# A Hymba layer on one core: halved RMS statistics, ScalarE sums for the first norm, respaced sums of the down weights and a hand-set GpSimd order

## The chip, the cores and the metric

The kernel is one launch on one core of a Trainium2 chip. The time is device microseconds from the start to the end of an execution, and lower is better. Engines are named as the profile names them: PE is TensorE (matmuls), DVE is VectorE, ACT is ScalarE, POOL is GpSimd, and SP issues the DMAs, one after the other in the order of its queue.

## What is computed

One layer on 1024 tokens of width 1024, in float32. Four steps follow one another: embedding norm and mixing (stick-breaking attention of 8 heads beside causal pooling of 4 windows), the first layer norm, a squared-ReLU feed-forward of width 4096 with the second norm, and a gated embedding with the third.

```python
x = layer_norm(x, emb_ln_g, emb_ln_b)
proj = x @ w_in; q, k, v, u = split(proj, [512, 1024, 1536])
o = stick_breaking_attention(q, k, v)              # 8 heads of 64
o = o * rsqrt(mean(o * o, per head) + 1e-6) * attn_out_g
pooled = multiscale_pool(u, w_pool, pool_scale)    # windows 2, 4, 8, 16
x = layer_norm(2**0.25 * x + concat(o, pooled) @ w_out, ln1_g, ln1_b)
h = square(relu(x @ w_up)) @ w_down
x = layer_norm(2**0.25 * x + h, ln2_g, ln2_b)
x = layer_norm(2**0.25 * x + sigmoid(x @ w_gate) * (p @ w_ple), ln3_g, ln3_b)
```

## The kernel before

A value enters a matmul as a high and a low part (`split`: ACT casts the high part at L65, DVE or POOL subtracts it at L66), and a product is three matmuls (`mm3`, L69 to L71). The stages follow one another in time.

**Attention, 110 to 384 us.** There are 64 tiles: 4 pairs of heads `pr`, 2 heads `j`, 8 blocks `t` of 128 queries. The loop over n has an order of PE that is written by hand. `weigh` (two z matmuls, two sigmoids on ACT at L398 and L399, a scan on DVE at L400, a multiply and a memset on POOL at L403 and L404) runs three tiles ahead of `turn` (transposes of the weights `aa`, L126, split into `ath` and `atl`) and, on every second tile, `gather` (matmuls `o`, L429). Between them stands the fill: projections `pq` in steps of three matmuls, and the pooling groups, which `pool_group` computes: matmuls `pp`, a scaled copy `y` on ACT (L494), 1 to 4 shifted adds `s` on POOL (L499), and the result `pooled` on DVE (L503 to L507). RATES says how much fill goes beside a tile: 0.37 for the first 48, 0.6 for the others. When a pair is complete its output gets its RMS norm: `rms_square` (one ACT square of 1024 columns, L441), `rms_stats` (matmuls `pm` L447, ACT L450, POOL power L451, POOL copy into `ms` L453) and `rms_apply` (transposes `pb` L460, DVE multiply L462). The fourth pair's stand after the loop, with the last fill around them. Pooled groups and pairs go to DRAM (`mspill`) and come back as `mraw`.

**Output weights, 384 to 484 us.** Three rounds take 3, 3 and 2 blocks of 128 tokens. Each round loads 8 row blocks of `w_out` through two slots: DMA into `wraw`, cast `wh` on ACT, remainder `wl` on DVE or POOL by `takes`, then matmuls `acc`. Round 0 also splits the mixed values (`mix`). After a round, each row block gets its first norm: `xr` from `acc` on DVE (L820), `bn_stats` and its aggregate on DVE (L97, L99, L101), a power on POOL (L103), two passes on DVE (L110, L113), transposes, a copy `xval` and splits (`normed`), and a store `rspill`.

**Start of the up phase, 484 to 530 us.** From here on the order of all engines is written by hand. Rows 6 and 7 get their norm (`finish_rows`, `norm_apply`) between the first products.

**Up phase, 530 to 810 us.** Sixteen groups `g` of seven products (`up`, 12 matmuls each; Strassen's way of seven). Beside each group, sums of the second weights are made for the phase behind: `down_fetch(m)` loads two tiles `draw`, `down_sums(m)` makes four sums on POOL (L574), `down_out(m)` stores them as `tspill`. All three are for group m = g, but group 3 does two, so that m runs one ahead from there. The two `draw` slots are shared, so the fetch of m+1 waits until the stores of m have landed. SP also stores the results `hid` (`hspill`) and loads the up weights `uraw`.

**Down phase, 810 to 1130 us, and the gate, to the end.** The gate phase has norms whose statistics are made on ACT (L1186 to L1189).

Of the kernel before, what the change touches and what calls it, by code (L numbers as in the profile page):

```python
# [8 lines left out]
F32 = mybir.dt.float32  # L9
# [25 lines left out]
def hymba_layer(ctx: ExitStack, tc: tile.TileContext, x, p, emb_g, emb_b, w_in, attn_g, w_pool,  # L35
# [70 lines left out]
    def norm_apply(src, dst, g, b, stats, done=None):  # L106
# [5 lines left out]
        for cs in parts:  # L112
            V.scalar_tensor_tensor(out=dst[:, cs], in0=dst[:, cs], scalar=rs, in1=b[:, cs],  # L113
                                   op0=ALU.mult, op1=ALU.add)
            if done:
                done(cs)

# [248 lines left out]
    RATES = (0.37, 0.6)  # L366
# [72 lines left out]
    def rms_square(pr):  # L439
        sq[pr] = slot("ra", "sq")  # L440
        A.activation(out=sq[pr], in_=oraw[pr], func=AF.Square)  # L441

    def rms_stats(pr):

        pm = bank("b6", "pm")[:, 0:2 * NT]
        for i in range(NT):
            T.matmul(pm[:, 2 * i:2 * i + 2], lhsT=sq[pr][:, i * P:(i + 1) * P], rhs=hm,  # L447
                     start=True, stop=True)
        rs = small.tile([P, 2 * NT], F32, name="rms", bufs=2)
        A.activation(out=rs, in_=pm, func=AF.Identity, bias=eps)  # L450
        G.tensor_tensor(out=rs, in0=rs, in1=mhalf, op=ALU.pow)  # L451
        ms[pr] = slot("K", "ms")
        G.tensor_copy(out=ms[pr].rearrange("p (n d) -> p n d", d=HD),  # L453
                      in_=rs.unsqueeze(2).broadcast_to([P, 2 * NT, HD]))

    def rms_apply(pr, c):
        cs = slice(c * CH, (c + 1) * CH)
# [4 lines left out]
        V.scalar_tensor_tensor(out=oraw[pr][:, cs], in0=oraw[pr][:, cs],  # L462
# [59 lines left out]
    with tc.manual_schedule(engines={mybir.EngineType.PE}):  # L522
        for n in range(-AHEAD, len(tiles)):
# [11 lines left out]
            else:  # L535
# [21 lines left out]
    def mix(k):  # L557
        both = big("mix")
        mixh[k], mixl[k] = both[:, 0:S], both[:, S:2 * S]
        raw = pooled[0] if k == 4 else oraw[3] if k == 3 else None  # L560
# [37 lines left out]
    def normed(i, tps):  # L598
# [4 lines left out]
        xval[i] = slot("ra" if i < 6 else "K", "xval")  # L603
# [177 lines left out]
    for r0 in range(0, NT, 3):  # L781
# [35 lines left out]
        for i in tiles:  # L817
# [4 lines left out]
            layer_norm(xr[i], xr[i], g1, b1)  # L822
# [122 lines left out]

    with tc.manual_schedule(engines=ALL):
# [3 lines left out]
        def finish_rows(i):  # L950
# [4 lines left out]
            stats[i] = norm_stats(xr[i])  # L955
# [32 lines left out]
        norm_apply(xr[6], xr[6], g1, b1, stats[6])  # L988
# [343 lines left out]
```

## Time and profile before

| | |
|---|---|
| Median of 3 runs | 1240.09 us (1237.65 to 1240.2) |
| Profiled execution | 1238.67 us, of which its span 1236.7 us |
| PE busy | 1163.7 us, 94% |
| DVE busy | 903.1 us, 73% |
| ACT busy | 599.2 us, 48% |
| POOL busy | 520.3 us, 42% |
| PE's granted clock, mean | 0.976 of 2.4 GHz |

The page gives busy time over the whole span, and it is a mean over stages with different limits. PE is near full in most of the 40 slices of the page, and shows lower digits and a lower clock in few. A busy PE at half clock (1.2 GHz) counts as busy, so idle time and clock have to be read together, stretch by stretch.

### The profile page before, as it was taken

What the parts mean: (1) busy time and instruction counts of PE and PEld (TensorE: products, weight loads), DVE (VectorE), ACT (ScalarE), POOL (GpSimd) and SP (SyncE); (2) the same over time, 40 slices, a digit from 0 to 9 for tenths busy, and PEclk for the clock granted to TensorE, in tenths of its full rate; (3) what the DMA queues carried; (4) which work ended last, traced back from release to release, by engine and by line L of the source; (5) the groups of instructions that cost most, each with busy time, mean ns of one, the idle gap of its engine ahead of it and who ended that gap; (6) DMA issues with size and microseconds to landing.
All of it is one profiled execution on the core that took longest, in us unless ns stands there. A gap on an engine that the chain in (4) does not pass through costs nothing.

```text
span 1236.7 us, 15529 instructions
## 1 busy us (share of the span) xinstructions
PE 1163.7 (94%) x5520; PEld 964.1 (78%) x5520; DVE 903.1 (73%) x1114; ACT 599.2 (48%) x1038; POOL 520.3 (42%) x368
## 2 busy tenths in 40 slices
PE   7999988899997998699899999999999999998997
PEld 5877877787876876588688888878888888887886
DVE  7735878796865678868576776768888887788565
ACT  5425756675644244454446455466333343335653
POOL 3211443354752236633342332336645564465332
PEclk9999999999997999799899999999999999999999
DMA  9824121121226363378778877799666655643122
GB/s 347 291 115 136 27 61 60 43 60 43 71 83 242 120 243 132 102 253 263 238 256 278 269 252 261 253 378 394 231 220 196 214 175 169 208 138 118 68 78 76
DMA packets 123580, 221.48 MB, mean 179 GB/s; under 512 B 9456, under 2 KB 64240, under 8 KB 123504
## 3 DMA queue, kind: packets, MB, share of 16 engines
q1 hardware_dynamic: 123504, 220.50, 52.4%
q8 instruction: 43, 0.70, 0.2%
q14 instruction: 33, 0.27, 0.1%
HBM read 148.12 MB, written 70.25 MB: 177 GB/s over the span
## 4 chain that ended last, share of the span: by engine, by line
PE 71%; DVE 10%; ACT 6%; DMA 5%; issue 5%; POOL 2%; SPq 1%; DVEq 0%; ACTq 0%; POOLq 0%
PE pd L69 8%; PE pd L71 7%; PE pd L70 7%; PE pu L70 6%; PE pu L71 6%; PE pu L69 6%; PE tp L126 3%; PE pq L69 3%; PE pq L70 3%; PE pq L71 2%; PE acc L70 2%; PE o L429 2%; DVE rr L400 2%; PE acc L71 2%; PE acc L69 2%
## 5 line engine op out<-in xcount | busy, mean ns | idle before, releaser
L574 POOL TENSOR_TENSOR draw<-draw 128x512 f32<-128x512 f32 x64 | 97.1, 1517 | 180.1 <-DMA draw<-in_w_down_dram 177.5
L890 DVE TENSOR_TENSOR xres<-xres,pd 128x512 f32<-128x512 f32 x208 | 137.4, 680 | 45.4 <-PE pd L71 44.5
L574 POOL TENSOR_TENSOR dop<-draw,dop 128x1024 fp32r<-128x1024 f32 (+1 forms) x48 | 112.1, 2355 | 125.2 <-ACT dop L866 107.1
L866 ACT CAST dop<-draw 128x1024 fp32r<-128x1024 f32 (+1 forms) x96 | 81.3, 905 | 134.8 <-DVE xres L890 51.4
L69 PE MATMUL pd<-dop 128*128 128x512 f32 x320 | 125.1, 391 | 2.0 <-DVE xres L890 1.9
L70 PE MATMUL pd<-dop 128*128 128x512 f32 x320 | 124.8, 390 | 0.1
L71 PE MATMUL pd<-dop 128*128 128x512 f32 x320 | 124.6, 389 | 0.0
L574 DVE TENSOR_TENSOR dop<-draw,dop 128x1024 fp32r<-128x1024 f32 (+1 forms) x48 | 85.6, 1784 | 3.6 <-ACT dop L866 3.6
L751 ACT COPY hid<-pu 128x512 f32<-128x512 f32 x48 | 28.2, 588 | 120.8 <-PE pu L71 69.0
L69 PE MATMUL pq<-xh,wh 128*128 128x512 f32 x192 | 77.9, 406 | 0.8 <-DVE ul L66 0.8
L400 DVE TENSOR_TENSOR_SCAN rr<-rr,diag 128x640 f32<-128x640 f32 (+3 forms) x32 | 71.3, 2228 | 9.5 <-ACT rr L398 8.6
L403 POOL TENSOR_TENSOR aa<-aa,rr 128x639 f32<-128x639 f32 (+3 forms) x32 | 56.9, 1779 | 48.4 <-DVE rr L400 48.4
L70 PE MATMUL pq<-xl,wh 128*128 128x512 f32 x192 | 76.7, 399 | 0.0
L71 PE MATMUL pq<-xh,wl 128*128 128x512 f32 x192 | 76.5, 398 | 0.0
L69 PEld LDWEIGHTS pd<-dop 128*128 128x128 f32 x320 | 60.0, 188 | 16.6 <-DVE xres L890 3.2
L574 DVE TENSOR_TENSOR hid<-pu,hid 128x512 f32<-128x512 f32 x48 | 33.0, 688 | 52.7 <-PE pu L71 37.8
L70 PEld LDWEIGHTS pd<-dop 128*128 128x128 f32 x320 | 60.1, 188 | 13.0 <-POOL dop L574 0.8
L71 PEld LDWEIGHTS pd<-dop 128*128 128x128 f32 x320 | 60.1, 188 | 12.5
L65 ACT CAST wh<-wraw 128x1024 fp32r<-128x1024 f32 x36 | 38.0, 1056 | 53.9 <-PE acc L70 26.2
L66 DVE TENSOR_TENSOR atl<-tp,ath 128x512 fp32r<-128x512 f32 (+2 forms) x96 | 50.7, 546 | 15.4 <-ACT ath L65 14.6
L70 PE MATMUL acc<-wl,mix 128*128 128x512 f32 x128 | 51.7, 404 | 4.2 <-POOL wl L66 4.2
L574 DVE TENSOR_TENSOR hid<-hid,hid 128x512 f32<-128x512 f32 x48 | 53.8, 1145 | 0.6
(253 smaller groups left out, 3359.3 us busy)
## 6 DMA issues: line engine op xcount, KB each, us to landing
hspill<-hid SPq DMA_DIRECT2D x48, 512.0 KB, 4.9
draw<-hspill SPq DMA_DIRECT2D x48, 512.0 KB, 6.0
uraw<-in_w_up_dram SPq DMA_DIRECT2D x32, 512.0 KB, 5.8
draw<-in_w_down_dram SPq DMA_DIRECT2D x32, 512.0 KB, 4.7
tspill<-draw SPq DMA_DIRECT2D x64, 256.0 KB, 4.2
wraw<-in_w_out_dram SPq DMA_DIRECT2D x24, 512.0 KB, 3.6
draw<-in_w_down_dram SPq DMA_DIRECT2D x48, 256.0 KB, 5.1
wraw<-in_w_in_dram SPq DMA_DIRECT2D x16, 512.0 KB, 4.9
```

The costliest lines, as they stand in the source:

```text
L65: A.copy(out=h, in_=src)
L66: (eng or V).tensor_tensor(out=l, in0=src, in1=h.bitcast(F32), op=ALU.subtract)
L69: T.matmul(ps, lhsT=lh, rhs=rh, start=start, stop=False, **kw)
L70: T.matmul(ps, lhsT=lh, rhs=rl, start=False, stop=False, **kw)
L71: T.matmul(ps, lhsT=ll, rhs=rh, start=False, stop=stop, **kw)
L126: T.transpose(tp[:, j * P:(j + 1) * P], src[:, (k0 + j) * P:(k0 + j + 1) * P], ident)
L400: V.tensor_tensor_scan(out=rr[:, 0:n][:, ::-1], data0=rr[:, 0:n][:, ::-1], data1=diag[:, S - n:S][:, ::-1], initial=0.0, op0=ALU.mult, op1 ...
L403: G.tensor_tensor(out=aa[:, 0:n - 1], in0=aa[:, 0:n - 1], in1=rr[:, 1:n], op=ALU.mult)
L574: eng.tensor_tensor(out=o, in0=i0, in1=i1, op=op)
L751: A.copy(out=quarter(g, name), in_=ups[g, "A"])
L866: A.copy(out=h, in_=raw)
L890: V.tensor_tensor(out=xres[i][:, cs], in0=xres[i][:, cs], in1=src, op=ALU.add)
```

## The change

In the attention, the RMS norm of each pair is done in two halves of 512 columns, the first after block 3 and the second after block 7 of the second head. The square comes one tile later, the statistics two, the multiply four. Of the fourth pair, the second half's `pm` and `pb` fall behind the first `acc` matmuls, and `mix(3)` is split by halves. RATES[1] goes from 0.6 to 0.8. POOL's order in the attention is written by hand. The first norm's statistics are made on ACT by `row_stats` (a sum by Identity, a mean, a sum by Square, a variance; POOL's power), with `xval` as scratch, and `bn_stats` go. In the up phase the sums of group m start every sixth product up to m = 7 and every seventh from there, and stores and the next fetch follow three products later. `act_stats` and `act_apply` of the gate phase call the new helpers.

```diff
+    def row_stats(src, unused, tag):
+        s1, nm, s2, var, rs = [small.tile([P, 1], F32, name=nme, tag=nme + tag)
+                               for nme in ("s1", "nm", "s2", "va", "ra")]
+        A.activation(out=unused, in_=src, func=AF.Identity, accum_out=s1)
+        A.activation(out=nm, in_=s1, func=AF.Identity, scale=-1.0 / D)
+        A.activation(out=unused, in_=src, func=AF.Square, bias=nm, accum_out=s2)
+        A.activation(out=var, in_=s2, func=AF.Identity, scale=1.0 / D, bias=lneps)
+        G.tensor_tensor(out=rs, in0=var, in1=mhalf[:, 0:1], op=ALU.pow)
+        return nm, rs
+    def row_apply(src, stats, g, b, step, cs=slice(0, D)):
...
-    RATES = (0.37, 0.6)
+    RATES = (0.37, 0.8)
...
+    def rms_square(pr, c):
+        if pr not in sq:
+            sq[pr], ms[pr] = slot("ra", "sq"), slot("K", "ms")
+        A.activation(out=sq[pr][:, half(c)], in_=oraw[pr][:, half(c)], func=AF.Square)
...
-    with tc.manual_schedule(engines={mybir.EngineType.PE}):
+    with tc.manual_schedule(engines={mybir.EngineType.PE, mybir.EngineType.Pool}):
...
-                if k.j == 1 and k.t == NT - 1:
-                    rms_square(k.pr)
-                    later.setdefault(n + 2, []).append((rms_stats, k.pr))
-                    later.setdefault(n + 8, []).append((rms_apply, k.pr, 0))
-                    later.setdefault(n + 10, []).append((rms_apply, k.pr, 1))
-        fill.run(4)
-        rms_stats(3)
+                if k.j == 1 and k.t in (3, 7):
+                    c = k.t // 4
+                    for m, f in ((1, rms_square), (2, rms_stats), (4, rms_apply)):
+                        later.setdefault(n + m, []).append((f, k.pr, c))
         fill.finish()
-        rms_apply(3, 0)
-        rms_apply(3, 1)
+        for n in sorted(later):
+            for f, *args in later[n]:
+                if f is not rms_apply:
+                    f(*args)
...
+        if k == 3:
+            for c in range(2):
+                if c:
+                    rms_apply(3, 1)
+                split(oraw[3][:, half(c)], mixh[k][:, half(c)], mixl[k][:, half(c)])
+            return
...
-            layer_norm(xr[i], xr[i], g1, b1)
+            xval[i] = slot("ra", "xval")
+            stats1 = row_stats(xr[i], xval[i], "1")
+            for step in range(2):
+                row_apply(xr[i], stats1, g1, b1, step)
...
+    sums_at = {6 * m if m < 8 else 7 * (m - 1): m for m in range(NG)}
+
+    def weight_sums(g, n):
+        n += 7 * g
+        if n in sums_at:
+            down_sums(sums_at[n])
+        if n - 3 in sums_at:
+            m = sums_at[n - 3]
+            down_out(m)
+            if m + 1 < NG:
+                down_fetch(m + 1)
...
-            stats[i] = norm_stats(xr[i])
+            xval[i] = slot("K", "xval")
+            stats[i] = row_stats(xr[i], xval[i], "1")
...
-                down_sums(m)
+                weight_sums(g, 0)
...
-            if m < NG:
-                down_out(m)
-            if m + 1 < NG:
-                down_fetch(m + 1)
+            weight_sums(g, 2)
...
-            if g == 3:
-                down_sums(4)
+            weight_sums(g, 5)
```

PE at the end of the attention, before: the low-part matmuls of the last gather, a fill step, the last pooling group, then both RMS steps of the fourth pair.

```order
L429 MATMUL o<-atl,vs 128x256 x7
L69 MATMUL pq<-xh,wh 128x512
L70 MATMUL pq<-xl,wh 128x512
L71 MATMUL pq<-xh,wl 128x512
L69 MATMUL pp<-uh,wph 128x512
L70 MATMUL pp<-ul,wph 128x512
L71 MATMUL pp<-uh,wpl 128x512
L69 MATMUL pp<-uh,wph 128x512
L70 MATMUL pp<-ul,wph 128x512
L71 MATMUL pp<-uh,wpl 128x512
L447 MATMUL pm<-hm,sq 128x2 x8
L460 MATMUL pb<-ident,ms 128x128 x8
```

After, from the statistics of the fourth pair's first half to the first `acc`: tiles 62 and 63 are transposed in one run.

```order
L474 MATMUL pm<-hm,sq 128x2 x4
L149 MATMUL tp<-ident,aa 128x128 x15
L452 MATMUL o<-ath,vs 128x256 x7
L452 MATMUL o<-ath,vs 128x128
L452 MATMUL o<-atl,vs 128x128
L452 MATMUL o<-atl,vs 128x256 x7
L485 MATMUL pb<-ident,ms 128x128 x4
L69 MATMUL acc<-wh,mix 128x512
```

What moved: 14 fill steps and the last two pooling groups went ahead of tile 61's transposes, and half of `pm` and `pb` went behind, so that no fill stands from there to the first `acc`.

POOL at the same place, before: tile 63's multiply (1023 columns) with the adds of the last two pooling groups, then the power and the copy.

```order
L403 TENSOR_TENSOR aa<-aa,rr 128x1023
L499 TENSOR_TENSOR s_3453<-s_3450 128x1020
L499 TENSOR_TENSOR s_3644<-y 128x1023
L499 TENSOR_TENSOR s_3647<-s_3644 128x1022
L499 TENSOR_TENSOR s_3736<-y 128x1023
L451 TENSOR_TENSOR rms<-rms,mhalf 128x16
L453 COPY ms<-rms 128x1024
```

After:

```order
L426 TENSOR_TENSOR aa<-aa,rr 128x1023
L427 MEMSET aa 128x1
L524 TENSOR_TENSOR s_3619<-y 128x1023
L524 TENSOR_TENSOR s_3622<-s_3619 128x1022
L524 TENSOR_TENSOR s_3690<-y 128x1023
L478 TENSOR_TENSOR rms<-rms,mhalf 128x8
L479 COPY ms<-rms 128x512
L478 TENSOR_TENSOR rms<-rms,mhalf 128x8
L479 COPY ms<-rms 128x512
L66 TENSOR_TENSOR wl<-wraw,wh 128x1024
```

What moved: the third add of the 8-window group is done earlier, three adds in a row stand between tile 63's multiply and the first power, and power and copy come in two halves.

ACT in the second round of the output weights, before: casts of the weights, then the copies and splits of row 0.

```order
L65 CAST wh<-wraw 128x1024 x11
L606 COPY xval<-tp 128x512
L65 CAST b11h<-tp 128x2x128
L606 COPY xval<-tp 128x512
L65 CAST b11h<-tp 128x2x128
```

After, with the statistics of rows 0 to 2 between the casts:

```order
L65 CAST wh<-wraw 128x1024 x3
L125 ACTIVATE xval,s_4057<-xr 128x1024
L65 CAST wh<-wraw 128x1024
L126 ACTIVATE nm<-s_4057 128x1
L125 ACTIVATE xval,s_4095<-xr 128x1024
L127 ACTIVATE xval,s_4059<-xr,nm 128x1024
L125 ACTIVATE xval,s_4133<-xr 128x1024
L126 ACTIVATE nm<-s_4095 128x1
L128 ACTIVATE va<-s_4059,lneps 128x1
L126 ACTIVATE nm<-s_4133 128x1
L65 CAST wh<-wraw 128x1024
```

What moved: six passes of 1024 columns, and their small ones, now stand on ACT around casts on which the round's matmuls wait.

SP in groups 2 to 4 of the up phase, before, from the store of group 2's second pair of results (`hid_5261`; `hid_5281` is its third, `hid_5157` and `hid_5233` are group 3's first and fourth):

```order
L74 DMA hspill<-hid_5261 128x1024
L74 DMA uraw<-in_w_up_dram 128x8x128
L74 DMA hspill<-hid_5281 128x1024
L74 DMA tspill<-draw 128x512 x4
L74 DMA draw<-in_w_down_dram 128x1024 x2
L74 DMA hspill<-hid_5157 128x1024
L74 DMA hspill<-hid_5233 128x512
L74 DMA tspill<-draw 128x512 x4
L74 DMA draw<-in_w_down_dram 128x1024 x2
L74 DMA uraw<-in_w_up_dram 128x8x128
```

After (`hid_5305` and `hid_5325` are group 2's second and third, `hid_5193` and `hid_5273` group 3's first and fourth):

```order
L74 DMA uraw<-in_w_up_dram 128x8x128
L74 DMA tspill<-draw 128x512 x4
L74 DMA draw<-in_w_down_dram 128x1024 x2
L74 DMA hspill<-hid_5305 128x1024
L74 DMA uraw<-in_w_up_dram 128x8x128
L74 DMA hspill<-hid_5325 128x1024
L74 DMA hspill<-hid_5193 128x1024
L74 DMA hspill<-hid_5273 128x512
L74 DMA tspill<-draw 128x512 x4
L74 DMA draw<-in_w_down_dram 128x1024 x2
L74 DMA uraw<-in_w_up_dram 128x8x128
```

What moved: the stores of m = 3 and the fetch of m = 4 stand ahead of group 2's second and third stores, and between the stores of m = 3 and of m = 4 there are now four stores and a load of up weights, where there were two stores.

## Rows read from the trace of the kernel before

**Rows 1.** Stretches: us, busy of PE, PEld, DVE, ACT, POOL (x instructions), PE's clock, DMA share.

```profile
349.99:384.65 34.66, 24.91 (x132) 20.68 (x130) 16.45 (x26) 14.05 (x28) 16.60 (x9) 0.86 0.56 192
418.00:484.00 66.00, 61.17 (x285) 49.08 (x285) 53.35 (x75) 27.08 (x43) 33.79 (x17) 1.00 0.57 199
506.00:530.00 24.00, 17.11 (x60) 13.44 (x59) 19.24 (x25) 14.44 (x26) 15.20 (x10) 0.64 0.47 156
610.00:622.00 12.00, 7.71 (x20) 5.69 (x21) 8.27 (x9) 7.00 (x11) 2.82 (x3) 0.57 0.80 281
622.00:810.00 188.00, 188.00 (x831) 155.65 (x831) 133.24 (x149) 95.86 (x146) 60.35 (x40) 1.00 0.79 263
```

**Rows 2.** Timeline of PE, attention's end: start, us, instruction [idle before, releaser].

```profile
347.24 0.39 PE L69 MATMUL pq<-xh,wh 128*128 128x512 f32 x1
...
349.99 0.93 PE L126 MATMUL tp<-ident,aa 128*128 128x128 f32 x6
...
374.49 3.12 PE L447 MATMUL pm<-hm,sq 128*128 128x2 f32 x16
382.53 1.97 PE L460 MATMUL pb<-ident,ms 128*128 128x128 f32 x8 [4.92 <-POOL ms L453]
```

**Rows 3.** Chain of work that ended last, 355 to 395: start, us, what.

```profile
375.64 7.88 DMA mraw<-mspill
```

**Rows 4.** Timeline of POOL, attention's end.

```profile
344.51 3.61 POOL L499 TENSOR_TENSOR s<-y 128x1023 f32<-128x1023 f32 x1
...
353.96 2.89 POOL L403 TENSOR_TENSOR aa<-aa,rr 128x1023 f32<-128x1023 f32 x1 [2.19 <-DVE rr L400]
356.81 1.88 POOL L499 TENSOR_TENSOR s<-s 128x1020 f32<-128x1020 f32 x1
...
378.00 3.38 POOL L451 TENSOR_TENSOR rms<-rms,mhalf 128x16 f32<-128x16 f32 x1 [0.65 <-ACT rms L450]
381.44 1.04 POOL L453 COPY ms<-rms 128x1024 f32<-128x1024 f32 x1
```

**Rows 5.** Timeline of DVE, attention's end.

```profile
350.71 3.17 DVE L400 TENSOR_TENSOR_SCAN rr<-rr,diag 128x1024 f32<-128x1024 f32 x1 [0.28 <-ACT rr L398]
...
364.45 1.29 DVE L66 TENSOR_TENSOR atl<-tp,ath 128x512 fp32r<-128x512 f32 x2 [1.87 <-ACT ath L65]
...
377.38 1.23 DVE L503 SCALAR_TENSOR_TENSOR pooled<-s,y 128x1024 f32<-128x1024 f32 x1 [3.04 <-POOL s L499]
```

**Rows 6.** Timeline of PE in the attention, behind the first pair's square.

```profile
238.02 0.33 PE L396 MATMUL z<-kh,qs 128*128 128x128 f32 x1 [2.14 <-ACT ra L399]
```

**Rows 7.** Groups of ACT instructions, gate phase: busy us, mean ns | idle before.

```profile
L1188 ACT ACTIVATE unused<-xres,nm 128x1024 f32<-128x1024 f32 x13 | 15.0, 1154 | 0.4
L1186 ACT ACTIVATE unused<-xres 128x1024 f32<-128x1024 f32 x13 | 13.9, 1071 | 14.9 <-DVE xres L1229 14.9
```

**Rows 8.** Groups of DVE instructions, 400 to 512, by form.

```profile
L97 DVE BATCH_NORM_STATS2 st<-xr 128x6 f32<-128x512 f32 x16 | 10.6, 677 | 0.0
```

**Rows 9.** Timeline of ACT in the second round of the output weights.

```profile
444.21 1.05 ACT L65 CAST wh<-wraw 128x1024 fp32r<-128x1024 f32 x1 [2.68 <-DMA wraw<-in_w_out_dram]
```

**Rows 10.** Timeline of PE, start of the up phase.

```profile
505.73 1.09 PE L126 MATMUL tp<-ident,xr 128*128 128x128 f32 x8 [1.91 <-DVE xr L113]
509.17 0.58 PE L69 MATMUL pu<-t2h,uh 128*128 128x256 f32 x1 [2.35 <-ACT t2h L638]
```

**Rows 11.** Timeline of SP's queue, groups 2 to 4 of the up phase.

```profile
579.29 0.32 SPq L74 DMA_DIRECT2D hspill<-hid  x1
...
603.00 0.38 SPq L74 DMA_DIRECT2D uraw<-in_w_up_dram  x1
```

**Rows 12.** Timeline of DVE, same groups.

```profile
610.80 1.59 DVE L574 TENSOR_TENSOR s<-uraw 128x512 f32<-128x512 f32 x1 [10.12 <-DMA uraw<-in_w_up_dram]
```

**Rows 13.** Timeline of ACT, same groups.

```profile
582.55 0.59 ACT L751 COPY hid<-pu 128x512 f32<-128x512 f32 x1 [3.59 <-DMA hspill<-hid]
```

**Rows 14.** Timeline of PE, same groups.

```profile
614.25 0.79 PE L69 MATMUL pu<-t2h,uh 128*128 128x512 f32 x1 [5.99 <-ACT uh L655]
```

More of the change, by code (lines that the diff above doesn't have):

```diff
@@ L116, in norm_apply @@
                 done(cs)
+    lneps = const.tile([P, 1], F32, name="lneps")
+    V.memset(lneps, LN_EPS)
+    def row_stats(src, unused, tag):
[8 more added lines that the diff above has]
+    def row_apply(src, stats, g, b, step, cs=slice(0, D)):
+        nm, rs = stats
+        if step == 0:
+            V.scalar_tensor_tensor(out=src[:, cs], in0=src[:, cs], scalar=nm,
+                                   in1=g[:, cs], op0=ALU.add, op1=ALU.mult)
+        else:
+            V.scalar_tensor_tensor(out=src[:, cs], in0=src[:, cs], scalar=rs,
+                                   in1=b[:, cs], op0=ALU.mult, op1=ALU.add)
     def layer_norm(src, dst, g, b, tag="", st=None, done=None):
@@ L437, in gather, with half, rms_stats @@
                         in0=o[0:HD, 0:2 * P], in1=ob, op=ALU.add)
[L439 to L449, printed above, removed]
+    def half(c):
+        return slice(c * CH, (c + 1) * CH)
+    def rms_square(pr, c):
+        if pr not in sq:
+            sq[pr], ms[pr] = slot("ra", "sq"), slot("K", "ms")
+        A.activation(out=sq[pr][:, half(c)], in_=oraw[pr][:, half(c)], func=AF.Square)
+    def rms_stats(pr, c):
+        pm = bank("b6", "pm")[:, 0:NT]
+        for i in range(4):
+            T.matmul(pm[:, 2 * i:2 * i + 2], lhsT=sq[pr][:, (4 * c + i) * P:(4 * c + i + 1) * P],
+                     rhs=hm, start=True, stop=True)
+        rs = small.tile([P, NT], F32, name="rms", bufs=2)
         A.activation(out=rs, in_=pm, func=AF.Identity, bias=eps)
[L451 to L454, printed above, removed]
+        G.tensor_tensor(out=rs, in0=rs, in1=mhalf[:, 0:NT], op=ALU.pow)
+        G.tensor_copy(out=ms[pr][:, half(c)].rearrange("p (n d) -> p n d", d=HD),
+                      in_=rs.unsqueeze(2).broadcast_to([P, NT, HD]))
     def rms_apply(pr, c):
-        cs = slice(c * CH, (c + 1) * CH)
         pb = bank("b6", "pb")
@@ L461, in rms_apply @@
                         ms[pr][:, (4 * c + i) * P:(4 * c + i + 1) * P], ident)
-        V.scalar_tensor_tensor(out=oraw[pr][:, cs], in0=oraw[pr][:, cs],
+        V.scalar_tensor_tensor(out=oraw[pr][:, half(c)], in0=oraw[pr][:, half(c)],
                                scalar=osc[:, pr:pr + 1], in1=pb, op0=ALU.mult, op1=ALU.mult)
@@ L559, in mix @@
         mixh[k], mixl[k] = both[:, 0:S], both[:, S:2 * S]
-        raw = pooled[0] if k == 4 else oraw[3] if k == 3 else None
+        if k == 3:
[4 more added lines that the diff above has]
+            return
+        raw = pooled[0] if k == 4 else None
         if raw is None:
@@ L987, in hymba_layer @@
         up(0, "p2")
-        norm_apply(xr[6], xr[6], g1, b1, stats[6])
+        for step in range(2):
+            row_apply(xr[6], stats[6], g1, b1, step)
         up(1, "p1")
@@ L991, in hymba_layer @@
         take(0, "a11", "C")
-        norm_apply(xr[7], xr[7], g1, b1, stats[7])
+        for step in range(2):
+            row_apply(xr[7], stats[7], g1, b1, step)
         up(1, "p2")
@@ L1040, in hymba_layer @@
             n1, n2 = g + 1 if g + 1 < NG else None, g + 2 if g + 2 < NG else None
-            m = g if g < 4 else g + 1
             if g:
@@ L1065, in hymba_layer @@
                 up_load(n2, 0)
+            weight_sums(g, 1)
             if not n1:
@@ L1090, in hymba_layer @@
                 up_s21(n1)
+                weight_sums(g, 3)
                 if g:
@@ L1176, in hymba_layer, with act_apply @@
     x2 = {}
[L1179 to L1180 removed]
     unused = []
     def act_stats(i, tag):
[L1184 to L1200 removed]
+        return row_stats(xres[i], unused[0], tag)
+    def act_apply(i, stats, *args):
+        row_apply(xres[i], stats, *args)
     def turn2(i):
```

24 lines of the change are left out of this document (2 added, 22 removed).

## The prediction

> **What bounds the kernel now.** First the busy times and the 40 slices of the page: PE is busy for 94% of the span, so the change can win only what PE idles or does at half clock. Then PE's busy time and granted clock by stretches [rows 1]: the losses lie together. From tile 61's transposes to the first `acc` PE is busy for 24.9 of 34.7 us at a mean clock of 0.86; at the start of the up phase for 17.1 of 24 at 0.64; in group 4 of the up phase for 7.7 of 12 at 0.57; in the output weights for 61.2 of 66 at full clock. Then, place by place, what ended PE's waits. At the attention's end it is POOL's copy `ms`, 4.92 us [rows 2], while the chain of waits goes through another wait that ends just as late, the load of `mraw`, 7.88 us from 375.64 on [rows 3]. Both must come earlier for the end to move. In the attention a square on ACT stands ahead of sigmoids and the z matmul waits 2.14 us [rows 6]. At the start of the up phase two waits, 1.91 and 2.35 us, follow row 7's norm [rows 10]. In group 4, 5.99 us, half clock behind it [rows 1, 14].
>
> The sum is made against the profiled execution, 1238.67 us, which is 1.4 us under the median of the runs.
>
> **A, the attention's end: -5.5 us, bounds 0 and -11.** Four fill steps take 2.75 us from 347.24 to 349.99, 0.69 each [rows 2], so the 14 that go ahead move tile 61's transposes to 349.99 + 9.6 = 359.6; call that T. What stays behind T is 24.9 busy [rows 1] less 9.6, less half of `pm` and of `pb` (3.12 and 1.97 [rows 2], so 2.5), 12.8 us. Without a wait the first `acc` would stand at 372.4, 12.3 us earlier than 384.65. But the fill that covered the chain from tile 63's scan is gone. Its steps go by these rows: before, the scan ends 3.9 us after the transposes and POOL's multiply 6.9 [rows 4, 5], of which 2.2 was the wait for the scan. So the multiply ends between T+4.7 and T+6.9; with less fill ahead of it I set T+5.5. Then three adds. Two rows of an add give 1.88 and 3.61 us [rows 4]. I take 1.9, since by the order DVE has only two remainders and then waits for these sums, so T+11.2; `pooled` of the 4-window group 1.2 [rows 5] beside the last add, its small ones, `pooled` of the last group at T+13.2, and only then DVE comes to the remainders `atl` of tiles 62 and 63, four at 0.65 [rows 5], and the last matmuls `o`: T+17.6. The power and the copy, 3.38 and 1.04 for the whole [rows 4], run beside that, ending by T+16. So `pb` and the first `acc` come at T+18.1, 377.7, which is 7.0 earlier. The half of `pm` and `pb` that went behind the first `acc` matmuls costs 1.4 (2.5 was at half clock in part). 7.0 less 1.4 is 5.5. The load of `mraw` must hold as well: by the order it now stands right behind the store of the last pooled group, at about T+12, and ahead of four loads of `xr`; it lands between 2 and 7.9 us later [rows 3], at T+14 to T+20. At its late end the gain is 2.
>
> By the Trainium skill, "GPSIMD Engine Reference", section "8. Key points", POOL shares its SBUF interfaces with VectorE and suffers from instructions with two SBUF inputs. The rows agree, like adds having taken 1.88 and 3.61 us [rows 4]; were all three contended, the first `acc` would come 5.2 us later and the gain would be 0.3. That is in rival 1.
>
> **B, the attention's body: -2, bounds +2 and -5.** Three pairs have their square in halves. The wait of 2.14 [rows 6] is behind a 1.06-us square; the half square comes a tile later, with half the length, where sigmoids are done. POOL's multiply now stands ahead of its memset of one column, which is near nothing either way. The group sums now stand in a run of four and one of three on POOL, 7.5 and 5.6 us [rows 4]: a tile's multiply behind a run can be late, though it is made three tiles ahead of its use. Both signs are thus open: +2 is one wait like that of 2.14, -5 takes two such waits with the clock behind them away.
>
> **C, the output weights: -1, bounds +4 and -4.** Per row, ACT gains two passes, 1.07 and 1.15 us [rows 7], and small ones on one column, and DVE loses two `bn_stats` at 0.68 [rows 8] and small ones. ACT is busy for 27 of 66 us here, DVE for 53 and POOL for 34 [rows 1], so work goes from the fuller engine to the emptier one. Yet on ACT the passes stand among casts `wh` on which the matmuls wait. Before, a cast waited 2.68 us for its DMA [rows 9]; one pass fits in that, two rows' don't. A row's norm ends earlier on DVE by 1.4 and later on ACT by 2.2, and the third row is the one that decides. SP has its loads ahead of the stores at a few places, which costs nothing while a cast waits for PE or DMA.
>
> **D, the start of the up phase: -3, bounds 0 and -6.** PE waits for DVE here: 1.91 for row 7's second pass, 2.35 for a split behind it [rows 10]. DVE loses four `bn_stats`, 2.7 us [rows 8], and four small ones; ACT, which does them instead, has little else (14.4 of 24 us from 506 on, less before) [rows 1]. Since DVE works without a gap up to these waits, what it loses goes over to PE nearly whole, and with the half clock behind the waits up to twice that. The bound 0 is the case that ACT's two passes, 2.2 us in a row, end later than the statistics that they replace, so that the norm starts no earlier.
>
> **E, group 4 of the up phase: -6, bounds -2 and -9.** SP has two groups of stores and fetches in group 3. The second stands ahead of a load `uraw`, which is issued at 603.00 and lands for DVE at 610.80 [rows 11, 12], and from that come the 5.99 [rows 14]. From 608.3 to 622 PE does what fills 4.6 us (20 matmuls at 0.23), so the loss is 9 with the clock [rows 1]. Changed, sums start each 6 products (16.3 us), with the stores three products behind, and between two sets of stores stand a `uraw` and four `hspill`. The load is no longer stuck. But the stores of m = 3 stand ahead of group 2's second `hspill`, which was issued at 579.29, and ACT's `keep` waited 3.59 us for it to land already [rows 11, 13]. That wait grows by about 4 us and costs PE some 2. Without it 9 less 1 of small waits, with all of it -2. I take 6.
>
> By the Trainium skill, "DMA: Bandwidth & Descriptors", "Anatomy of one DMA — SWDGE (gpsimd) path", a semaphore's wait happens on the issuing sequencer before dispatch, so a store that waits holds up what is queued behind it. Rows 11 and 12 agree: the load came out late, not slowly alone. By that rule the spread still has one blocked place; the price is in rival 1.
>
> The sum: -5.5 - 2 - 1 - 3 - 6 = -17.5, so 1221.2 for a profiled execution, and 1222.6 as a median.
>
> **The rivals.**
> Rival 1, the covers are gone: the adds on POOL are contended, or `mraw` lands late, and A gives nothing; E gives 2, the stall having moved to group 3, where SP is held up by the stores of m = 3. B 0, C 0, D -3: 1233.7, as a median about 1235. For it speaks that no fill is left behind T; against it, that by the order DVE is empty beside two of the adds.
> Rival 2, everything comes free: A -10, B -4, C -1, D -5, E -9, in sum -29, as a median 1211. For it: PE is busy for 188 of the 188 us behind group 4 at full clock [rows 1], and a wait that goes takes its half clock along. Against it: each place has a next wait in line.
> Rival 3, slower: ACT's statistics become the bound of the output weights. Their place is ahead of the casts of rounds 2 and 3; the price is 2.2 us for each of 6 rows, 13.3, and half again for the clock that falls behind each wait (in group 4 a wait of 6 cost 9 [rows 1, 14]), 20 in all. With -16.5 of the others +3.5, as a median 1243.6. It decides from the point where casts wait for ACT rather than for DMA, that is when more than 2.7 us of passes stand in one gap. Against it speaks ACT's idle 39 of 66 us.
>
> **How the numbers follow.** The forecast has 0.55, rival 1 0.20, rival 2 0.15, rival 3 0.06; its mild end, where the price is 17 and eats up the 16.5, has 0.04 and lies within 0.2% of before, about what a measurement of this kernel can tell from no change. So faster 0.90, same 0.04, slower 0.06. The terms' bounds give more than the range can use, since they won't all fall on one side: with about half of each side's for the forecast, 1214 to 1231. The range has to leave 2 in 10 out at most, so it takes in rival 1 and most of rival 2: 1210 to 1236.
>
> **What would show it.** A: the first `acc` at 376 to 380, the idle before `pb` under 1 us, POOL's three adds at 1.9, and DVE's `pooled` of the last group ahead of the last `atl`; an add at 3.6 or a cast `mix` that waits for `mraw` is rival 1. B: no 2-us wait of z for ACT. C: PE's idle time in the second and third rounds no more than 5 us; casts that wait for their engine's own passes are rival 3. D: the waits behind row 7's norm shorter by 2 to 3 us in sum. E: no wait of 5 us or half clock in group 4, a `keep` in group 3 that waits for `hspill` up to 8 us. The forecast is wrong if the up phase has a new wait in each of its first groups, or if PE stands still in the output weights.

## The result

The changed kernel takes 1225.88 us (median of 4 runs, 1224.69 to 1228.29) against 1240.04 us for the kernel before in the runs beside it. The ratio is 0.9893, with a 95% interval of 0.9872 to 0.9914: 14 us, or 1.1%, faster. The forecast was 1222.6 within 1210 to 1236.

The profiled execution took 1228.29 us, the longest of the four, so the traces below show 10.4 us of the 14. Read it first by stretches, as in [rows 1]: the end of the attention from tile 61's transposes to the first `acc`, the twelve microseconds of half clock, the output weights, the start of the up phase, and group 4.

```profile
358.40:377.19 18.79, 12.54 (x77) 11.09 (x76) 12.65 (x17) 7.88 (x16) 11.36 (x7) 0.91 0.55 183
376.00:388.00 12.00, 12.00 (x60) 10.25 (x60) 11.11 (x12) 10.20 (x13) 1.14 (x1) 0.96 1.04 392
418.00:484.00 66.00, 58.48 (x269) 47.05 (x268) 43.76 (x51) 38.99 (x74) 33.14 (x16) 0.97 0.54 183
500.00:530.00 30.00, 22.59 (x91) 18.01 (x89) 24.13 (x30) 19.25 (x33) 16.74 (x12) 0.83 0.55 175
600.00:612.00 12.00, 8.05 (x28) 5.90 (x27) 8.46 (x9) 7.19 (x11) 2.85 (x2) 0.86 0.76 274
```

The second of these stretches in the kernel before:

```profile
376.00:388.00 12.00, 6.93 (x24) 5.77 (x25) 4.76 (x6) 4.25 (x5) 5.76 (x3) 0.50 1.04 398
```

The first `acc` comes 18.8 us after tile 61's transposes, at 377.2 instead of 384.65. Behind it the clock stays high: from 376 to 388 it is 0.96, where it was 0.50 before. In the output weights ACT rose from 27.1 to 39.0 us of 66 and DVE fell from 53.4 to 43.8, yet PE is busy for 58.5, less than the 61.2 before. Group 4 keeps part of its stall. (What is called group 4's stall stands, by PE's order, ahead of the first product of group 5, whose weights are loaded beside group 4.)

Where the time went is best told by PE's own landmarks, since its instructions are nearly the same in all kernels. The table gives the start of the first `acc`, and then four lengths: to group 0's first half product with `t2`; from there to group 2's product with `t2`; from group 4's product with `t2` to group 7's with `b22`; and from there to the last matmul. From group 2 to group 4 all kernels take 38.1 us.

| kernel | median us, ratio to before (95%) | first acc | weights | start of up | groups 4 to 7 | rest |
|---|---|---|---|---|---|---|
| before | 1240.04 | 384.65 | 114.1 | 52.2 | 82.9 | 556.5 |
| changed | 1225.88, 0.989 (0.987 to 0.991) | 377.2 | 116.0 | 50.2 | 80.0 | 556.6 |
| control (changed again) | 1228.31, 0.989 (0.985 to 0.993) | 376.7 | 115.3 | 50.2 | 83.1 | 556.1 |
| old_sums | 1230.65, 0.991 (0.988 to 0.995) | 374.3 | 116.5 | 49.4 | 83.3 | 557.7 |
| bn_early | 1223.26, 0.985 (0.982 to 0.988) | 374.5 | 116.6 | 46.7 | 80.8 | 556.3 |
| bn_late | 1229.74, 0.991 (0.988 to 0.994) | 376.6 | 116.9 | 52.3 | 80.0 | 557.9 |
| rate06 | 1238.48, 1.000 (0.998 to 1.001) | 387.3 | 116.6 | 50.7 | 80.3 | 556.2 |
| rate_alone | 1245.26, 1.007 (1.004 to 1.011) | 391.3 | 117.2 | 47.9 | 82.0 | 556.7 |
| load_first | 1224.59, 0.988 (0.986 to 0.990) | 377.2 | 116.2 | 49.4 | 77.8 | 557.3 |
| row7_late | 1219.95, 0.984 (0.981 to 0.987) | 374.5 | 110.3 | 48.1 | 79.3 | 556.4 |
| bn_lf | 1219.56, 0.985 (0.983 to 0.988) | 376.9 | 112.8 | 47.2 | 76.2 | 557.7 |
| row7_lf | 1216.74, 0.982 (0.980 to 0.985) | 378.3 | 110.3 | 48.1 | 74.7 | 556.8 |
| best | 1214.78, 0.981 (0.979 to 0.984) | 375.6 | 110.3 | 48.8 | 74.4 | 557.6 |
| best_bn | 1217.67, 0.982 (0.979 to 0.984) | 377.1 | 113.0 | 47.2 | 75.6 | 557.7 |

So in the profiled execution the change won 7.5 us up to the first `acc`, lost 1.9 in the output weights, won 2.0 at the start of the up phase and 2.9 in groups 4 to 7. These lengths scatter, and single ones have to be read with care: before and rate_alone have the same code in the weights and the start of the up phase, and take 114.1 and 52.2 us against 117.2 and 47.9; bn_early and bn_lf, again the same, take 163.3 and 160.0 for the two together. The 1.9 and the 2.0 lie inside that scatter, and the two stages together took 166.2 us, as good as the 166.3 before. Three points were open: why the weights lost, why group 4 kept a stall, and what in the attention's end carries the gain.

### The profile page after: what moved, and what is told of

It reads as the page before. It is cut to its first block, busy times and chain, and to the rows that moved or that the text cites. A ratio compares the mean times of both kernels' runs of the same rounds, so it can differ in the third digit from the quotient of the medians.

```text
span 1226.5 us, 15593 instructions
## 1 busy us (share of the span) xinstructions
PE 1160.8 (95%) x5520; PEld 962.7 (78%) x5520; DVE 898.0 (73%) x1083; ACT 620.8 (51%) x1095; POOL 519.4 (42%) x376
## 4 chain that ended last, share of the span: by engine, by line
PE 66%; DVE 10%; DMA 8%; ACT 6%; issue 5%; POOL 3%; SPq 1%; DVEq 0%; POOLq 0%; ACTq 0%
PE pd L69 8%; PE pd L70 8%; PE pd L71 7%; PE pu L71 5%; PE pu L70 5%; PE pu L69 5%; PE tp L149 3%; PE pq L69 3%; PE pq L71 2%; PE pq L70 2%; PE o L452 2%; DMA tspill<-draw 2%; DVE rr L423 2%; PE acc L69 2%; PE acc L70 2%
## 5 line engine op out<-in xcount | busy, mean ns | idle before, releaser
L71 PE MATMUL pq<-xh,wl 128*128 128x512 f32 x192 | 76.2, 397 | 0.0
L426 POOL TENSOR_TENSOR ra<-ra 128x127 f32<-128x127 f32 (+3 forms) x32 | 25.2, 788 | 91.6 <-DVE ra L423 85.0
L66 DVE TENSOR_TENSOR atl<-tp,ath 128x512 fp32r<-128x512 f32 (+2 forms) x96 | 50.7, 544 | 11.0 <-ACT ath L65 10.5
L65 ACT CAST ath<-tp 128x512 fp32r<-128x512 f32 (+2 forms) x96 | 45.1, 484 | 24.1 <-PE tp L149 23.1
```

The costliest lines, as they stand in the source:

```text
L65: A.copy(out=h, in_=src)
L66: (eng or V).tensor_tensor(out=l, in0=src, in1=h.bitcast(F32), op=ALU.subtract)
L71: T.matmul(ps, lhsT=ll, rhs=rh, start=False, stop=stop, **kw)
L426: G.tensor_tensor(out=aa[:, 0:n - 1], in0=aa[:, 0:n - 1], in1=rr[:, 1:n], op=ALU.mult)
```

## The experiments

### The sums in their old places, and the change once more

`old_sums` has everything but the spread:

```diff
     def weight_sums(g, n):
-        n += 7 * g
-        if n in sums_at:
...
+        m = g if g < 4 else g + 1
+        if n == 0:
+            down_sums(m)
+        elif n == 2:
...
+        elif n == 5 and g == 3:
+            down_sums(4)
+        elif n == 6 and g == 3:
+            down_out(4)
+            down_fetch(5)
```

> The change with the old places of the sums of the down weights (two sets in group 3). Theory 1, by the two traces side by side: the spread brought 2.9 us between group 3 and group 5, so this kernel is 3 us slower than the changed one, within 1.5. The forecast's term E said 6 (2 to 9). Rival (the spread only moved the stall): within 1 us of the changed kernel.

> The changed kernel itself, run again as the measure for the runs beside it. Theory 1 (its remaining wait in group 4 of the up phase, 3.43 us in the first trace, is built into SP's order): a wait of 2.5 to 4.5 us with ACT's uh as the releaser stands in this trace too, at the same product. Rival (the wait is an accident of one execution, whose time of 1228.29 was the highest of four): no PE wait over 1 us in group 4 here, and a time near 1225.

Measured: 1230.65 against 1228.31; the difference, 2.3, is inside the intervals. Groups 4 to 7 take 83.3 us; the other two kernels with the sums in their old places take 82.9 (before) and 82.0 (rate_alone), and of the six traces with the spread as changed five take 79.3 to 80.8, and the control's 83.1. So the spread is worth 0 to 3 us, not 6. The control's wait stands at the same product as in the first trace (2.42 us instead of 3.43, releaser ACT's uh), so it is built in. How it comes about is seen on four engines of the changed kernel: first SP, then DVE and PE.

```profile
586.65 1.80 SPq L74 DMA_DIRECT2D tspill<-draw  x4
592.51 1.07 SPq L74 DMA_DIRECT2D draw<-in_w_down_dram  x2
593.70 0.38 SPq L74 DMA_DIRECT2D uraw<-in_w_up_dram  x1
```

```profile
600.96 0.84 DVE L605 TENSOR_TENSOR s<-uraw 128x512 f32<-128x512 f32 x1 [8.12 <-DMA uraw<-in_w_up_dram]
```

```profile
604.60 0.50 PE L69 MATMUL pu<-t2h,uh 128*128 128x512 f32 x1 [3.43 <-ACT uh L685]
```

The stores `tspill` of m = 4 were issued by 588.45, the fetch `draw` waits for them to land until 592.5, and the `uraw` for the stalled product stands behind it, as in [rows 11, 12], only 9 us earlier while PE needs it 7.6 us earlier. From its issue it takes another 7.2 us to land (7.8 before). Ahead of that the control's ACT waited for another `uraw`, which was issued at 577.67 behind the stores of m = 3 and their fetch and took 8.6 us to land; PE lost 1.88 us to it, at 587.85:

```profile
586.27 1.04 ACT L685 CAST uh<-uraw 128x1024 fp32r<-128x1024 f32 x1 [5.03 <-DMA uraw<-in_w_up_dram]
```

### Loads ahead of the stores

```diff
-        if n - 3 in sums_at:
-            m = sums_at[n - 3]
+        wait = 4 if n in (22, 28) else 3
+        if n - wait in sums_at and n not in (21, 27):
+            m = sums_at[n - wait]
             down_out(m)
```

The stores of m = 3 and m = 4, and the fetches behind them, come four products after their sums instead of three.

> The change with the stores of m = 3 and m = 4 and the fetches behind them one product later, so that group 2's second hspill and group 4's uraw stand ahead of them on SP. Theory 1 (the wait of 2.4 to 3.4 us in group 4 and the 1.9 us for ACT's keep in group 3 come from waits ahead in SP's order): both waits under 0.5 us, no half clock there, and 4 to 7 us faster than the changed kernel. Rival (the loads are late because the DMA engines are full there, 0.99 busy in the first trace): the uraw lands as late, less than 2 us faster.

Measured: 1224.59. By the ratios to the kernel before (0.988 against the control's 0.989) that is 1 us, by the medians 4, and inside the intervals: the expected 4 to 7 are not shown in time. In the trace both waits are gone (from 580 to 600 PE is busy for all 20.00 us, and PE has no wait over 0.35 us between 520 and 620), and groups 4 to 7 take 77.8 us, 5.3 less than the control and 2.2 less than the first trace. The load is issued 10 us earlier:

```profile
583.50 0.38 SPq L74 DMA_DIRECT2D uraw<-in_w_up_dram  x1
589.66 2.02 SPq L74 DMA_DIRECT2D tspill<-draw  x4
```

At group 5's product with `b22` the gain was 9 us on the control (6 on the first trace), of which 4 were given back one group on: there the next `uraw` stands behind the stores of m = 5 (PE waits 1.26 us at 620.76). In row7_lf and best only about 1 is given back, and the stretch takes 74.4 to 74.7. The same edit takes 4.6 us out of these groups twice more, from bn_early to bn_lf and from row7_late to row7_lf. So it was the order on SP that made the wait. The rival, full DMA engines, falls as its cause: from 580 to 600 they were 0.79 busy, and 0.80 in the changed kernel, and this `uraw` took 8.7 us to land, more than the 7.2 there. That a load needs 7 to 9 us stays, which is why its place in the queue counts.

### The first norm by bn_stats, early and late rows

`bn_early` puts `layer_norm(xr[i], xr[i], g1, b1)` back for rows 0 to 5, `bn_late` puts `norm_stats` and `norm_apply` back for rows 6 and 7.

> The change with the first norm of rows 0 to 5 by bn_stats on DVE again; rows 6 and 7 stay on ACT. Theory 2, by the two traces side by side: ACT's statistics put a store of row 3 and a load of row 7 ahead of a w_out load in SP's order, SP waits 6.7 us for that store to land, and PE lost 2.0 us net over the stage; so this kernel is 1 to 3 us faster than the changed one and a cast wh of the third round waits no more than 4.5 us. The forecast's term C said that the statistics on ACT bring 1 us, so this kernel would be 1 us slower. Rival: the third round loses the same either way (within 1 us).

> The change with the norm of rows 6 and 7 by bn_stats on DVE again; rows 0 to 5 stay on ACT. Theory 3, by the two traces side by side: between the first half product of group 0 and the start of group 1 PE won 2.7 us, of which 0.7 were given back; so this kernel is 2 to 3 us slower than the changed one. The forecast's term D said 3 (0 to 6). Rival (the gain there comes from what arrives earlier, not from DVE's four bn_stats): within 1 us.

Measured: bn_late 1229.74, 1.4 us over the control, less than expected and inside the intervals. Its weights and start of the up phase take 169.2 us together, against 165.5 to 166.2 in changed, control and load_first, whose code there differs in this alone: taking the four `bn_stats` off DVE is worth about 3 us over the two stages. That is no more than two traces of one code differ by; that all three lie below speaks for it. PE's idle time in the start of the up phase hardly moved, though; what fell is the time at half clock. Here it is from the first `t2` to group 2, before, changed and in bn_late:

```profile
498.75:551.00 52.25, 42.50 (x186) 34.77 (x185) 40.58 (x46) 25.09 (x43) 26.66 (x17) 0.84 0.54 177
```

```profile
493.16:543.40 50.24, 40.58 (x184) 33.48 (x185) 41.25 (x45) 25.58 (x44) 29.76 (x19) 0.90 0.56 183
```

```profile
493.41:545.80 52.39, 42.28 (x186) 34.58 (x185) 39.97 (x46) 25.14 (x43) 27.22 (x17) 0.84 0.56 178
```

PE is idle for 9.75 us of the first, 9.66 of the second and 10.11 of the third. The wait for row 7's second pass is gone; in the changed kernel one for POOL's `t1l` is new, and that for `t2l`, 1.04 us before, is longer:

```profile
498.10 0.39 PE L70 MATMUL pu<-t1l,uh 128*128 128x256 f32 x1 [2.25 <-POOL t1l L605]
...
505.00 0.58 PE L70 MATMUL pu<-t2l,uh 128*128 128x256 f32 x1 [2.00 <-DVE t2l L605]
```

bn_early is 1223.26, 5 us under the control, more than the expected 1 to 3. Its weights and start of the up phase take 163.3 us against 165.5, 2.2 less, as expected; another 2.2 come before the first `acc` and 2.3 in groups 4 to 7, which the edit does not touch. The cast of the third round waits 4.48 us, as said. The waits of the changed kernel's third round tell the rest: SP's wait, then ACT's and PE's.

```profile
SPq L74 <- DMA rspill<-xr: 6.7, 1, 6.7
```

```profile
468.55 1.99 ACT L65 CAST wh<-wraw 128x1024 fp32r<-128x1024 f32 x2 [7.14 <-DMA wraw<-in_w_out_dram]
```

```profile
469.65 2.08 PE L69 MATMUL acc<-wh,mix 128*128 128x512 f32 x4 [2.62 <-ACT wh L65]
...
472.23 0.66 PE L69 MATMUL pu<-b11h,uh 128*128 128x512 f32 x1
...
484.74 0.39 PE L70 MATMUL acc<-wl,mix 128*128 128x512 f32 x1
```

SP waits for row 3's store to land before it can load row 7 into that buffer, and the last load of w_out stands behind. The last 8 `acc` matmuls stand behind 20 matmuls of the up phase (472.23, 484.74); why the scheduler, which orders the engines wherever the kernel does not, put them there, no run shows. PE has work in front of them, but row 6's norm can't start before them. In bn_early no up matmul stands ahead of an `acc`.

### Row 7's load behind the last weights

```diff
-                load(xr[i + 3], xspill[i + 3])
+                if i + 3 < 7:
+                    load(xr[i + 3], xspill[i + 3])
...
         if final:
+            load(xr[7], xspill[7])
             x_high("t2", 0, 1)
```

> The change with the load of row 7's residual issued after the last w_out load instead of ahead of it. The statistics stay on ACT. In PE's order the last 8 matmuls of the output weights, which in the changed kernel stand behind 20 matmuls of the up phase, then stand behind 2. Theory 2 (the ACT statistics cost by what they do to the order of the last loads and matmuls, and so to the start of row 6's norm): row 6's residual sum starts 3 to 5 us earlier than in the changed kernel (484.3 in the control's trace), and the time is 3 to 5 us shorter, as with bn_stats (1223.3 in the first batch). Rival (they cost by ACT's own passes ahead of the casts): within 1.5 us of the changed kernel.

Measured: 1219.95, 6 us under the changed kernel's first runs and, by the ratios to the kernel before, under the control too, with ACT's statistics kept; 3 to 5 were expected. The weights take 110.3 us, here and in the two other kernels with this edit, 5.7 less than in the changed kernel and 3.8 less than before. Row 6's residual sum starts 11.3 us earlier, 2.7 of them from the earlier first `acc` of this trace; here are the changed kernel's row and, behind it, row7_late's, on DVE:

```profile
485.39 1.29 DVE L1000 SCALAR_TENSOR_TENSOR xr<-xr,acc 128x512 f32<-128x512 f32 x2 [3.06 <-PE acc L71]
```

```profile
474.14 1.27 DVE L1002 SCALAR_TENSOR_TENSOR xr<-xr,acc 128x512 f32<-128x512 f32 x2
```

So the statistics on ACT did not cost by their passes, which are all still there. What cost was the order that came with them: one DMA in SP's queue and eight matmuls in PE's stood where they hurt. Both moved in this run, so their shares are not separated.

### The fill rate: with and without the rest

`rate06` is the change with `RATES = (0.37, 0.6)`; `rate_alone` is the kernel before with `RATES = (0.37, 0.8)`.

> The change with the fill rate of the last pair back at 0.6. Theory 4 (the gain at the attention's end comes from the fill that went ahead of tile 61, as term A had it): the first acc comes 3 to 6 us later than in the changed kernel's traces (377.2 and 376.7), and the time is 3 to 6 us longer. Rival (it comes from pm and pb of the last half going behind the first acc, and from the halved statistics): the first acc within 1.5 us of the changed kernel's.

> The kernel before with the fill rate of the last pair at 0.8 and nothing else. Theory 4 (the fill ahead of tile 61 is worth much only where pm and pb of the last half stand behind the first acc and mraw is loaded early): POOL's ms still ends the wait of pb, mraw still stands behind four loads of xr, the first acc comes less than 5 us earlier than in the kernel before, and the time is 1 to 5 us shorter. Rival (the rate does it alone): the first acc 7 to 10 us earlier, the time 9 to 13 us shorter.

Measured: rate06 1238.48, no different from the kernel before (ratio 1.000, 0.998 to 1.001), and rate_alone 1245.26, slower (1.004 to 1.011). Neither wins anything at the attention's end without the other, and together they bring the first `acc` from 384.65 to 377. Both expectations missed: without the rate the first `acc` comes 10 us later than in the changed kernel, not 3 to 6, and the rate alone costs 5 to 8 us where 1 to 5 were to be won. In rate06 `pb` waits 4.23 us for POOL's `ms`, and then the first `acc` 3.41 us for ACT's split of `mraw`, which waited for its load:

```profile
386.23 1.04 ACT L65 CAST mix<-mraw 128x1024 fp32r<-128x1024 f32 x1 [7.35 <-DMA mraw<-mspill]
```

SP issued that load at 378.38, behind four loads of `xr`, a `uraw` and a `wraw`, as in [rows 3]; in the changed kernel it went out at 369.92, right behind the last store, and landed by 375.68. In rate_alone the RMS norm of the whole pair follows the last gather, with no fill to cover it, at half clock (0.50 from 381.43 to the first `acc`):

```profile
381.43 3.58 PE L447 MATMUL pm<-hm,sq 128*128 128x2 f32 x16 [2.00 <-ACT sq L441]
389.46 1.97 PE L460 MATMUL pb<-ident,ms 128*128 128x128 f32 x8 [4.46 <-POOL ms L453]
```

The fill may go ahead only if the norm at the end no longer needs its cover, and the halved norm pays only if the last pooling group, and with it the loads of `mraw`, come earlier. Which part the halves of the norm, the place of the second half and POOL's order by hand each have in this, no run separates: none of them was taken back by itself.

### Two edits together, and the add on DVE

`row7_lf` has row 7's load and the later stores; `bn_lf` the later stores with bn_early's edit. `best` is row7_lf with the last group's one add moved (its line is the same in `best_bn`, which has bn_lf's edits instead):

```diff
-            G.tensor_tensor(out=s2[:, n:], in0=s[:, n:], in1=s[:, 0:S - n], op=ALU.add)
+            (V if g == 0 else G).tensor_tensor(out=s2[:, n:], in0=s[:, n:], in1=s[:, 0:S - n], op=ALU.add)
```

> Rows 0 to 5 by bn_stats and the later stores together. Theory: the two add, since they lie in different stages: 1223.3 less 4 to 7, so 1216 to 1219. Rival: the second kernel's gain is the DMA's, not the order's, and 1222 to 1223 remains.

> Row 7's load after the last w_out load, and the later stores of m = 3 and m = 4, together. Theory 1 and 2 (two waits in SP's order in different stages): 1219.95 less 2 to 5, so 1215 to 1218, and the wait in group 4 is gone as in the trace of the later stores alone. Rival (an earlier start of the up phase meets the same transfers sooner, so that the second edit gives nothing more): within 1.5 us of 1220.

> The same two edits, and the one add of the last pooling group on DVE instead of POOL. Theory 5 (at the attention's end the chain is tile 63's multiply, three adds on POOL, two pooled on DVE, then the remainders of tiles 62 and 63): without the third add, which took 2.33 us and waited 0.68, the first acc comes 1 to 2.5 us earlier against tile 61's transposes than in the changed kernel (18.8 us), and the time is 1 to 2 us under that of the two edits alone. Rival (mraw's landing or PE's own work is late next): less than 1 us earlier.

> The later stores of m = 3 and m = 4 and the add on DVE, as in the fastest kernel so far, but with the first norm of rows 0 to 5 by bn_stats on DVE instead of ACT's statistics with row 7's load behind. Theory 2: with SP's and PE's order mended, ACT's statistics take 1 to 4 us out of the output weights and the start of the up phase, so this kernel is 1 to 4 us slower than 1214.8. Rival (what counts is the order alone, and the engine of the statistics does not): within 1 us.

Measured: bn_lf 1219.56, just above the expected 1216 to 1219; row7_lf 1216.74; best 1214.78, the fastest, and 2.0 under row7_lf, inside the intervals; best_bn 1217.67. By the lengths the two edits of order add up: row7_lf has the 110.3 of the one and takes 4.6 us less in groups 4 to 7 than row7_late. The ratios show no more than a trend (0.984 to 0.982, and 0.985 for both bn_early and bn_lf). Whether ACT's statistics are worth anything with the order mended stays open within the intervals: best_bn's ratio, 0.9817 (0.9791 to 0.9842), holds that of best, 0.9814 (0.9789 to 0.9838). By the landmarks ACT's statistics take 2.7 us out of the weights (110.3 against 113.0) and lose 1.6 at the start of the up phase.

The add on DVE is not settled either. It takes 1.22 us there instead of 2.33 on POOL, and the wait of tile 63's transposes shrinks from 2.85 to 2.18, but the first `acc` stands 18.8 us behind tile 61's transposes in both, since PE's clock was lower in this trace: 0.51 from 369.5 to the first `acc`, and 0.66 from 372 on in the changed kernel's. In row7_lf, from which best differs by the add alone, it is 20.5 us; in the nine traces of the change's code there it lies between 18.8 and 20.5. This is best's PE row (8 transposes took 1.07 us in the changed kernel):

```profile
369.73 1.94 PE L149 MATMUL tp<-ident,aa 128*128 128x128 f32 x8 [2.18 <-DVE pooled L532]
```

## Why the prediction was right, and where it was not

**A, the attention's end: right; B can't be told from the scatter.** The forecast had tile 61's transposes at 359.6, the first `acc` 18.1 us behind, at 377.7. Measured: 358.40, 18.8, 377.2. The chain is the one that was named, as PE, POOL, DVE, ACT and, last, PE's clock show:

```profile
358.40 0.82 PE L149 MATMUL tp<-ident,aa 128*128 128x128 f32 x6
...
365.16 0.50 PE L69 MATMUL pp<-uh,wph 128*128 128x512 f32 x1 [3.16 <-DVE ul L66]
...
372.00 1.07 PE L149 MATMUL tp<-ident,aa 128*128 128x128 f32 x8 [2.85 <-DVE atl L66]
```

```profile
359.54 2.00 POOL L426 TENSOR_TENSOR aa<-aa,rr 128x1023 f32<-128x1023 f32 x1 [4.40 <-DVE rr L423]
...
361.54 1.89 POOL L524 TENSOR_TENSOR s<-y 128x1023 f32<-128x1023 f32 x1
363.50 2.75 POOL L524 TENSOR_TENSOR s<-s 128x1022 f32<-128x1022 f32 x1
366.93 2.33 POOL L524 TENSOR_TENSOR s<-y 128x1023 f32<-128x1023 f32 x1 [0.68 <-ACT s L525]
```

```profile
362.18 2.33 DVE L66 TENSOR_TENSOR wl<-wraw,wh 128x1024 fp32r<-128x1024 f32 x1 [1.50 <-ACT wh L65]
```

```profile
375.68 1.04 ACT L65 CAST mix<-mraw 128x1024 fp32r<-128x1024 f32 x1 [1.94 <-DMA mraw<-mspill]
```

```profile
372.00:377.00 5.00, 4.76 (x26) 4.52 (x27) 1.92 (x5) 2.15 (x4) 0.00 (x0) 0.66 0.98 349
```

Two misses inside cancel. The multiply ended at T+3.1, not T+5.5, for it took 2.0 us instead of 2.89 [rows 4]. And of three adds two were slower than 1.9, at 2.75 and 2.33, the first of these beside DVE's 2.33-us remainder `wl`, which began at 362.18. By the Trainium skill ("GPSIMD Engine Reference", "8. Key points") POOL contends with DVE instructions that have two SBUF inputs. The trace agrees in part: the add that began at 361.54 took 1.89, though `wl` ran beside it for two thirds of that. The third add also waited for ACT's copy. An added wait, 3.16 us for `ul`, was in no row, and from 372 to 377 PE ran at 0.66 of its clock, which the forecast had not counted. The step that "costs 1.4" for `pm` and `pb` behind the first `acc` was right: 9.2 us won at the twelfth `acc` were 7.8 after they had run. What had made 9.2 of the 7.5 at the first `acc` is the clock, which was half behind it before and full now; the forecast did not count it. Of B's 2 us the transposes show 1.2, by which they came ahead of 359.6, and that is less than traces of one code differ by; its one named place came out as said: z waits 0.53 us where [rows 6] had 2.14.

```profile
237.18 0.33 PE L419 MATMUL z<-kh,qs 128*128 128x128 f32 x1 [0.53 <-ACT ra L422]
```

What the forecast did not say is that the gain is a joint one (rate06, rate_alone).

**C, the output weights: -1 forecast, +1.9 measured, and the failed step is "SP has its loads ahead of the stores at a few places, which costs nothing while a cast waits for PE or DMA".** The +1.9 by itself is inside the scatter. But the order cost: a load stood behind a store's landing, 6.7 us, with w_out's last load behind it, the cast for that load waited 7.14 us, and with the one load moved (and PE's order with it) the weights took 5.7 us less. The rows for it were not in the trace of before, but the order of SP's queue, and of PE's, would have shown it. The reasoning on ACT's passes, one in each gap of 2.68 us, was not what decided.

**D, the start of the up phase: -3 forecast, -2.0 measured**, with -2.1 by bn_late's landmarks, and about -3 over this stage and the one before it. The size holds; with the order mended it is 3.4 to 4.1 against before, though row 6's norm then starts earlier too. The mechanism holds in half: the waits behind row 7's norm were to be "shorter by 2 to 3 us in sum", and PE's idle time stayed (9.75 and 9.66 us). The gain came with the clock, 0.84 before and 0.90 after, which the forecast had only as an addition.

**E, group 4: -6 forecast, 0 to -2.9 measured, and the failed step is "The load is no longer stuck".** The forecast blamed only the stores of m = 3. But those of m = 4 stood in front of the same load as before, with a fetch that waits for their landing: `draw` was issued at 592.51, four microseconds behind the last `tspill`. By the Trainium skill ("DMA: Bandwidth & Descriptors", "Anatomy of one DMA — SWDGE (gpsimd) path") a wait is kept by the issuing sequencer before dispatch, and the trace agrees; the forecast had cited the rule and applied it to one of two places. What was foreseen of group 3 came in the control only, and in another form: ACT stood 5.03 us before a cast of `uraw`, and its `keep` came late behind that.

The sum erred by 3 us by the medians and by 7 between the two profiled executions: C and E missed by 3 each and D by 1, while the attention, with 7.5 forecast in A and B, won 7.5 at the first `acc`. That the medians came nearer was luck as far as the terms go: the executions without a trace were up to 3.6 us faster, and no run shows where. Three of the nine traces with the change's code up to there had won 10 us at the first `acc`, by the clock after 110 us (last section), which is no term of the forecast. Of the rivals, 1 holds for E in part (the stall was moved within SP's queue), not for A. Rival 3, ACT's passes as the bound, did not come; what the weights lost, they lost at a smaller price and by another mechanism.

## What to carry to other kernels

When stores and loads share a queue that issues in order, write down for each load that the bound engine needs what waits in front of it; a store's landing that frees a buffer is such a wait, here 4.1 us of SP's time (`draw`) and 6.7 (row 7). A change of an engine's work can move instructions that it does not touch: compare the whole order of every queue, and look where the last matmuls of a stage went. A cover (fill) and the chain that it covers are changed together or not at all.

## What was not expected of the hardware

The same instructions up to the first `acc` took between 374.3 and 378.3 us in nine traces of the changed kernel and its variants with that same code; three of them (old_sums, bn_early, row7_late) lie at 374.3 to 374.5, the others at 376.6 and more. Between the changed kernel and row7_late 1.5 us are there before 115 us; as much again comes with the clock between 110 and 150 us, which was 1.00 in those three and 0.96 in all others. These are the stretch in the changed kernel and, below, in row7_late:

```profile
110.00:150.00 40.00, 37.04 (x206) 31.76 (x206) 32.15 (x40) 27.48 (x64) 14.33 (x22) 0.96 0.24 62
```

```profile
110.00:150.00 40.00, 37.01 (x217) 31.55 (x217) 33.83 (x40) 29.62 (x68) 15.90 (x24) 1.00 0.19 51
```

One trace on each side can thus mislead by 3 to 4 us, which is as much as terms C, D or E; lengths between landmarks are safer, but not free of it. The clock at the attention's end differed too: behind waits of 2 to 3 us it was 0.66 in the changed kernel's trace and 0.51 in best's. And behind a wait for the same `ul`, 1.95 us in bn_early and 1.93 in bn_lf, whose code is the same up to there, it fell in the first and stayed in the second:

```profile
478.00:483.00 5.00, 4.00 (x11) 3.15 (x12) 4.21 (x6) 4.04 (x10) 0.00 (x0) 0.66 0.00 0
```

```profile
478.00:483.00 5.00, 3.82 (x17) 3.18 (x18) 4.39 (x6) 4.04 (x9) 0.00 (x0) 1.00 0.00 0
```

No run here shows on what that hangs.
